# Where twelve modulation rows are loaded and summed in a decoder layer: convolution anchors, other buffers, three later sums

## The chip, the cores and the metric

The kernel runs on one core of a Trainium2 chip. The metric is device time in microseconds (us) for one execution of the whole layer. The engines of the core work side by side, each through its own list of instructions in a fixed order: PE (matrix products), DVE and POOL (elementwise), ACT (elementwise with functions; its queue also issues transfers), SP (issues transfers). An instruction that waits holds up all that stand behind it on its engine.

## The reference

One decoder layer for a sequence of 512 positions with 1024 channels, in float32. Cut to what matters here:

```python
mod = silu(c) @ ada_w + ada_b                       # c: 1024 -> 6 * 1024
sh1, sc1, g1, sh2, sc2, g2 = split(mod, 6)

u = rms_norm(x, mix_pre_g) * (1 + sc1) + sh1
qk_raw, v, o_pre, gates, glu = split(u @ w_in)
q, k = split(silu(causal_dwconv(qk_raw, width 4)))
h = mlstm_chunkwise(q, k, v, gates)                 # 4 heads of 256, chunks of 128
h = rms_norm(h, ml_norm_g) * sigmoid(o_pre)
y = silu(layer_norm(causal_dwconv(glu, width 31)))
mix = concat(h, y) @ w_out
x = x + g1 * rms_norm(mix, mix_post_g)

u = rms_norm(x, ffn_pre_g) * (1 + sc2) + sh2
a, gt = split(causal_dwconv(u @ ffn_up, width 3))
x = x + g2 * rms_norm((silu(gt) * a) @ ffn_down, ffn_post_g)
```

The change concerns `mod` alone: when its parts g1, sh2 and sc2 are computed, and from which buffers.

## The kernel before

**The products.** Every float32 matrix product is done as three products of rounded parts: a matrix is split into a high part (a rounding, on ACT, the names that end in h) and a low part, the remainder (a subtraction, on POOL or DVE, the names that end in l). `w_split` does this for the weights `wqko` and `wvo` of a head, `wo` of the output projection and `wup` of the FFN, 512 columns at a time. PE runs high x high, low x high and high x low.

**The stages.** In the opening x is normed and turned, and the first 16 modulation rows are made. Then the loop `for h in range(H - 1)` goes over heads 0 to 2: attention of head h is a generator `steps`, and between its steps head h+1 is projected. `head_proj(h + 1, i)` for i = 0 to 3 makes two tiles of q and two of k (`q_0c`, `q_1c`, `k_2c`, `k_3c`): products into a PSUM bank `qko`, then a convolution of four taps (the first on ACT, L562, three on DVE, L564) and a silu on ACT (L565). `make_vo(h + 1)` makes v and the output gate. `make_E(h + 1)` makes the decay matrices `E` with seven exps on ACT; DVE multiplies them with the scores `s` (L653). Calls of `pace()` in between run a part of the width-31 convolution (`cv`, `cs`). After the loop come attention of head 3 and the norm of the convolution branch (`ry_s` on PE, `ry_t` on DVE, `ry_r` on POOL), then the output projection by a scheme of few products (banks `mixa`, `mixb`; operands `mku`, `m`, `mt`, `ms`), and last the FFN with up and down projection, from about 400 us to the end.

**The modulation rows.** The 6144 values of `mod` are 48 rows of 128 values: row i is a tile of weights, 128 partitions x 1024, times silu(c) (in `cb`), summed along 1024. `ada_load(i)` issues the transfer of 512 KB on ACT's queue, and `ada_sum(i)` is one DVE instruction, a product with a running sum (L191, its output tile is called `junk`). Rows 0 to 15 are done in the opening. Rows 16 to 23 are g1, rows 24 to 39 are sh2 and sc2, and rows 40 to 47 are g2 and are done in the FFN. `ada_done(a, b)` adds the bias to a group of rows, and `gains` are worked out from it for the norms.

**Where rows are put.** A small pool `adas` has two buffers of one row. From row 24 on rows also go to other tiles that lie idle: four slots of `spare` (a large tile, free when the last projection of a head has been read), half tiles of a side buffer (30 and 31) and two wide tiles (34 and 35). A load has to wait for the sum that reads the row that was in the buffer before.

**What sets the order.** PE and SP run in the order of the program. ACT, DVE and POOL are ordered by a scheduler that simulates the kernel; `behind(ins, anchor)` pins an instruction behind another of the same engine, and `tc.cur_priority += LATER` lets it yield to others. Inside `with in_order():`, which holds the output projection, the order is again the program's. `last_e[0]` is the last tap issued, `last_left[0]` the last of a head's remainders.

Of the kernel before, what the change touches and what calls it, by code (L numbers as in the profile page):

```python
# [13 lines left out]
AF = mybir.ActivationFunctionType  # L14
# [3 lines left out]
P = 128  # L18
D = 1024
# [3 lines left out]
H = 4  # L23
# [34 lines left out]
def decoder_layer(ctx, tc, w_glu0, x, c, adaT, vecs, w_glu, w_qko, w_v0, w_vo, w_mq, w_out, w_up, w_down, out):  # L58
    nc = tc.nc
# [112 lines left out]

    def ada_load(i):

        if 24 <= i < 28 or i in (32, 33, 36, 37):
            q = 2 * (i % 4 if i < 36 else i - 34)
            r = spare[0][:, q : q + 2, :].rearrange("p j t -> p (j t)")
        elif 30 <= i < 32:
            if i % 2 == 0:
                spare.append(side(f"ada_{i}"))  # L180
            r = spare[-1][:, (i % 2) * D : (i % 2 + 1) * D]
        elif i in (34, 35):
            r = (wide1 if i == 34 else wide2)[:, :D]
        else:
            r = adas.tile([P, D], F32, tag="ada", name=f"ada_{i}")
        nc.scalar.dma_start(r, adaT[i // 2][:, (i % 2) * D : (i % 2 + 1) * D])
        ada_rows[i] = r

    def ada_sum(i):
        junk = small.tile([P, D], BF16, tag="junk", bufs=1, name=f"junk_{i}")  # L190
# [2 lines left out]
    def ada_block(i, anchor):  # L193
        ada_load(i)
        behind(ada_sum(i), anchor)
# [362 lines left out]
    def conv4(ps, i, name):  # L558

        t = slot(f"{name}c")  # L560
        w = lambda tap: vcol("qk_conv_w", tap * 16 + i)
        S.activation(t, ps, AF.Identity, bias=vcol("qk_conv_b", i), scale=w(3))  # L562
        for d in range(1, 4):
            last_e[0] = V.scalar_tensor_tensor(out=t[:, d:], in0=ps[:, : T - d], scalar=w(3 - d), in1=t[:, d:], op0=ALU.mult, op1=ALU.add)  # L564
        S.activation(t, t, AF.Silu)  # L565
        return t

    hy = [None] * (2 * KT)

    heads = {}  # L570
# [31 lines left out]
    last_left = [None]  # L602
# [131 lines left out]
        return [three[s][:, a : a + n] for (s, a), n in zip(PLACE, NS)]  # L734

    E = [None] * H

    LO = 32
    Mhl = const.tile([P, T], F32R, name="Mhl")
# [6 lines left out]
    def make_E(h):  # L746
        mb = atbank(f"Mb{h}")
        PE.matmul(mb, pick[:, h : h + 1].to_broadcast([P, P]), Mhl, start=True, stop=True)
        md = slot(f"Md{h}")
        V.tensor_tensor(out=md.rearrange("p (t m) -> p t m", t=NT), in0=mb.rearrange("p (t m) -> p t m", t=NT),  # L750
                        in1=cmask[:, None, :].to_broadcast([P, NT, P]), op=ALU.add)
        E[h] = head_tiles(f"E{h}", F32)
        for cc in range(NT):
            b = ga[:, cc, h : h + 1]
            S.activation(E[h][cc][:, :P], md[:, cc * P : (cc + 1) * P], AF.Exp, bias=b, scale=-1.0)
            if cc < NT - 1:
                S.activation(E[h][cc][:, P:], mb[:, (cc + 1) * P :], AF.Exp, bias=b, scale=-1.0)
    head_load(0)
    head_proj(0, 0)
    head_proj(0, 1)  # L760
# [193 lines left out]
    def pace():  # L954
        tc.cur_priority += LATER
        next(paced, None)
        tc.cur_priority -= LATER
# [33 lines left out]
    def norm_split(a, b):  # L991
        for j in range(a, b):
# [2 lines left out]
            last_yl[0] = V.tensor_tensor(out=lo, in0=ys[j], in1=hi.bitcast(F32), op=ALU.subtract)  # L995
            hy[KT + j] = (hi, lo)

    def ada_pair(i):
        tc.cur_priority += LATER
        for n in range(i, i + 2):  # L1000
            behind(ada_sum(n), last_e[0])
        tc.cur_priority -= LATER

    for h in range(H - 1):
        for i in range(16 + 2 * h, 18 + 2 * h):
            ada_load(i)
        head_load(h + 1)
        steps = attention(h)
        if h == 0:
            head_proj(1, 0)  # L1010
            ada_pair(16)
            next(steps)
            head_proj(1, 1)
            pace()
            next(steps)
            pace()
            head_proj(1, 2)
            pace()
            next(steps)
        else:  # L1020
            next(steps)
            ada_pair(16 + 2 * h)
            if h == H - 2:
                for i in range(22, 24):
                    ada_load(i)
            head_proj(h + 1, 0)
            pace()
            for _ in turns:
                pass
            head_proj(h + 1, 1)  # L1030
            pace()
            next(steps)
            pace()
            head_proj(h + 1, 2)
            pace()
            next(steps)
        head_proj(h + 1, 3)
        if h == H - 2:
            ada_pair(22)
            ada_done(16, 24)  # L1040
            gain(0, 16, "mix_post_g")
        values = make_vo(h + 1)
        pace()
        next(steps)
        pace()
        next(values)
        next(steps)
        pace()
        next(values)
        if h == 0:  # L1050
            next(steps)
            pace()
        make_E(h + 1)
        if h == H - 2:
            norm_mean()
        next(values)
        if h < H - 2:
            turns = steps
        else:
            for _ in steps:  # L1060
                pass
        next(values)
        if h == H - 2:
            norm_sums()
# [1 line left out]
    spare.append(upool.tile([P, KT, T], F32, tag="ul", name="spare"))  # L1066
    tc.cur_priority += LATER
    for i in range(24, 26):
        ada_block(i, last_left[0])
    for i in range(26, 30):  # L1070
        ada_load(i)
    tc.cur_priority -= LATER
# [93 lines left out]
    with in_order():  # L1166
        wt1 = right_split(wt1)
        for i in range(2):
            wo_split(r8, NP - 2, i)
        for _ in steps:  # L1170
            pass
        for i in range(35, 40):
            ada_sum(i)
        for p in range(PAIRS):
            mix_product("s1", wt1, banks[:2], p, True)
        for t, ps in zip(ku3, banks):
            V.tensor_tensor(out=t, in0=ps, in1=t, op=ALU.subtract)
        for t, ps in zip(ku2, banks):
            V.tensor_tensor(out=ps, in0=ps, in1=t, op=ALU.subtract)
        we = wo1_load(0, EARLY)  # L1180
        g1r = row(0, lambda n: [wide1[:, :T], wide1[:, T : 2 * T]], "g1", nc.sync)
        we = wo1_split(we, 0, EARLY)
        w22 = right_split(w22, slots, "t")
        for n in range(NP - 2, NP):
            mix_first(n)
        for n in range(EARLY):
            mix_plain(n, banks, we[n], (2, 3), n == 0)
        wo = wo1_split(wo1_load(EARLY, EARLY + 4), EARLY, EARLY + 4)
        for tt, ps in enumerate(mixa):
            V.tensor_tensor(out=mg[tt], in0=ps, in1=g1r[0], op=ALU.mult)  # L1190
            sq_sum(ps, msq[:, 2 * tt : 2 * tt + 1], f"mixa{tt}")
        for p in range(PAIRS):
            mix_product("s4", w22, banks[:2], p)
        for t, ps in zip(ku3, banks[2:]):
            V.tensor_tensor(out=ps, in0=ps, in1=t, op=ALU.add)
        for n in range(EARLY):
            mix_plain(n, banks, we[n], (0, 1))
        wo += wo1_split(wo1_load(EARLY + 4, NP), EARLY + 4, NP)
    ada_done(24, 40)
    V.scalar_tensor_tensor(out=gains[:, KT : 2 * KT], in0=sc2[:, :, 0], scalar=1.0, in1=vcols("ffn_pre_g", 0, KT), op0=ALU.add, op1=ALU.mult)  # L1200
    V.tensor_scalar(out=gains[:, KT : 2 * KT], in0=gains[:, KT : 2 * KT], scalar1=RD, scalar2=None, op0=ALU.mult)
# [477 lines left out]
```

## Time and profile before

| | |
|---|---|
| time before, median of 3 runs | 773.56 us (773.38 to 774.5) |
| the profiled execution | 773.63 us |
| its span, first to last instruction | 771.9 us |
| granted PE clock, mean | 0.998 of full speed |
| engines' busy share of the span | PE 98%, DVE 76%, POOL 71%, ACT 56% |
| bytes moved | 154.92 MB, mean 201 GB/s |
| modulation rows on ACT's queue, to the `ada` buffers | 22 transfers of 512 KB |
| sums of those rows | 22, 37.3 us of DVE, mean 1.70 us |

The span is what lies between the first and the last instruction recorded; the execution takes 1.7 us more. An engine's busy share is over the whole span. Idle time of DVE, ACT or POOL says little by itself, since PE has nearly none. In a row of the timeline stand the start in us, the duration, the engine, the line, the operation, and output<-inputs with their shapes; in brackets the engine's idle time just ahead and what ended it. "ACTq" is the issue of a transfer on ACT's queue. PE's waits are listed as us in total, number of times, and longest.

### The profile page before, as it was taken

How to read it: one execution, taken by the hardware profiler on the slowest of the kernel's cores; microseconds unless marked ns; L12 is line 12 of the kernel's file. 1: busy time of each engine (PE TensorE's matmuls, PEld its weight loads, DVE VectorE, ACT ScalarE, POOL GpSimd, SP SyncE). 2: the span in 40 equal slices, each digit the busy share in tenths (PEclk: the TensorE clock that was granted, in tenths of full speed). 3: DMA queues.
4: the chain of work that ended last, by engine and by line, in shares of the span. 5: the costliest groups of instructions: out<-in, count | busy, mean ns of one | idle time of the engine just before them, and what ended most of it. 6: DMA issues, size and time to landing. Idle time of an engine off the chain costs nothing.

```text
span 771.9 us, 10261 instructions
## 1 busy us (share of the span) xinstructions
PE 753.5 (98%) x3485; PEld 622.6 (81%) x3485; DVE 587.5 (76%) x866; ACT 428.5 (56%) x823; POOL 546.3 (71%) x443
## 2 busy tenths in 40 slices
PE   7999999999999989999999999999999999999996
PEld 5878898878777778778878988888888888888885
DVE  6769899989969986578978887774774776654547
ACT  7584429775745665485348644443445355566643
POOL 5789759995683962857931077886986885599943
PEclk9999999999999999999999999999999999999999
DMA  8994854231141233666663765857667474796263
GB/s 319 351 401 159 164 151 164 110 109 56 56 163 55 94 126 109 233 198 211 217 253 122 252 218 203 310 185 269 249 245 287 149 279 170 266 398 245 102 239 143
DMA packets 41976, 154.92 MB, mean 201 GB/s; under 512 B 3954, under 2 KB 5378, under 8 KB 32772
## 3 DMA queue, kind: packets, MB, share of 16 engines
q1 hardware_dynamic: 28052, 101.57, 36.5%
q10 hardware_dynamic: 12272, 49.56, 17.9%
q0 software_dynamic: 1600, 3.15, 2.4%
q8 instruction: 27, 0.44, 0.2%
q14 instruction: 25, 0.20, 0.1%
HBM read 134.19 MB, written 26.35 MB: 208 GB/s over the span
## 4 chain that ended last, share of the span: by engine, by line
PE 64%; DVE 15%; DMA 6%; POOL 5%; issue 5%; ACT 4%; DVEq 0%; SPq 0%; POOLq 0%; ACTq 0%
PE up L229 31%; PE dn L229 13%; PE glu L229 7%; DVE cv L917 6%; PE mixb L229 4%; DVE junk L191 3%; PE vo L229 3%; DMA wglu<-in_w_glu 3%; DMA spare<-in_adaT 2%; PE qko L229 1%; PE v L229 1%; POOL cs L913 1%; DMA wvo<-in_w_vo 1%; PE glu L366 1%; PE mixa L229 1%
## 5 line engine op out<-in xcount | busy, mean ns | idle before, releaser
L917 DVE SCALAR_TENSOR_TENSOR cv<-gt,cvw,cv 128x502 f32<-128x502 f32 (+23 forms) x200 | 136.7, 730 | 3.0 <-ACT cv L905 1.8
L913 POOL TENSOR_TENSOR cs<-cs,cs 128x510 f32<-128x510 f32 (+3 forms) x32 | 44.0, 1374 | 1.0 <-ACT cs L911 0.7
L191 DVE SCALAR_TENSOR_TENSOR junk<-ada,cb 128x1024 bf16<-128x1024 f32 x22 | 37.3, 1698 | 4.5 <-DMA ada<-in_adaT 4.2
L211 POOL TENSOR_TENSOR wup_0l<-wup,wup_0h 128x512 fp32r<-128x512 f32 x18 | 26.0, 1447 | 19.1 <-ACT wup_0h L210 19.1
L229 PE MATMUL up<-u2h,wup_1024h 128*128 128x512 f32 (+1 forms) x96 | 35.8, 373 | 0.0
L229 PE MATMUL up<-u2l,wup_512h 128*128 128x512 f32 (+1 forms) x96 | 35.7, 372 | 0.0
L229 PE MATMUL up<-u2h,wup_0h 128*128 128x512 f32 (+1 forms) x96 | 35.7, 372 | 0.0
L229 PE MATMUL up<-u2l,wup_0h 128*128 128x512 f32 (+1 forms) x96 | 35.7, 372 | 0.0
L229 PE MATMUL up<-u2h,wup_0l 128*128 128x512 f32 (+1 forms) x96 | 35.7, 372 | 0.0
L229 PE MATMUL up<-u2h,wup_1536l 128*128 128x512 f32 (+1 forms) x96 | 35.6, 371 | 0.0
L229 PE MATMUL up<-u2h,wup_512h 128*128 128x512 f32 (+1 forms) x96 | 35.6, 371 | 0.0
L229 PE MATMUL up<-u2h,wup_1536h 128*128 128x512 f32 (+1 forms) x96 | 35.6, 371 | 0.0
L229 PE MATMUL up<-u2l,wup_1536h 128*128 128x512 f32 (+1 forms) x96 | 35.6, 371 | 0.0
L229 PE MATMUL up<-u2h,wup_512l 128*128 128x512 f32 (+1 forms) x96 | 35.6, 371 | 0.0
L229 PE MATMUL up<-u2l,wup_1024h 128*128 128x512 f32 (+1 forms) x96 | 35.6, 371 | 0.0
L229 PE MATMUL up<-u2h,wup_1024l 128*128 128x512 f32 (+1 forms) x96 | 35.6, 371 | 0.0
L911 ACT ACTIVATE cs<-gt,cvw 128x511 f32<-128x511 f32 (+4 forms) x40 | 27.3, 714 | 11.3 <-POOL cs L913 6.2
L211 POOL TENSOR_TENSOR wup_1536l<-wup,wup_1536h 128x512 fp32r<-128x512 f32 x18 | 25.3, 1406 | 5.2 <-ACT wup_1536h L210 5.2
L1412 DVE TENSOR_TENSOR b<-b 128x512 f32<-128x512 f32 x11 | 19.4, 1762 | 9.4 <-POOL b L1411 9.4
L346 DVE SCALAR_TENSOR_TENSOR junk<-ada,cps 128x1024 bf16<-128x1024 f32 x16 | 19.5, 1220 | 8.7 <-DMA ada<-in_adaT 7.9
L1411 POOL TENSOR_TENSOR b<-b 128x512 f32<-128x512 f32 x11 | 14.7, 1334 | 15.3 <-DVE b L1410 15.3
L210 ACT ACTIVATE wup_512h<-wup 128x512 fp32r<-128x512 f32 x22 | 13.8, 627 | 19.8 <-POOL fq L1468 11.3
(1267 smaller groups left out, 2787.8 us busy)
## 6 DMA issues: line engine op xcount, KB each, us to landing
wup<-in_w_up SPq DMA_DIRECT2D x22, 1024.0 KB, 5.3
ada<-in_adaT ACTq DMA_DIRECT2D x22, 512.0 KB, 5.6
b<-in_w_down ACTq DMA_DIRECT2D x11, 1024.0 KB, 6.2
spill_t<-b ACTq DMA_DIRECT2D x11, 1024.0 KB, 4.0
wqko<-in_w_qko SPq DMA_DIRECT2D x9, 1024.0 KB, 4.7
ada<-in_adaT SPq DMA_DIRECT2D x16, 512.0 KB, 7.2
wvo<-in_w_vo SPq DMA_DIRECT2D x6, 1024.0 KB, 4.8
wglu<-in_w_glu SPq DMA_DIRECT2D x5, 1024.0 KB, 6.6
```

The source lines that it names most:

```text
L191: return V.scalar_tensor_tensor(out=junk, in0=ada_rows.pop(i), scalar=1.0, in1=cb, op0=ALU.mult, op1=ALU.mult, accum_out=mod[:, i : i + 1])
L210: S.activation(hi[:, :n], src, AF.Copy)
L211: last_w[0] = (eng or G).tensor_tensor(out=lo[:, :n], in0=src, in1=hi[:, :n].bitcast(F32), op=ALU.subtract)
L229: PE.matmul(ps, l, r, start=start and i == 0, stop=stop and i == 2, skip_group_check=again)
L346: V.scalar_tensor_tensor(out=junk, in0=first[k][:, i * D : (i + 1) * D], scalar=1.0, in1=cps, op0=ALU.mult, op1=ALU.mult, accum_out=part[: ...
L366: PE.matmul(ps, blk(wk, i)[a], u[k][b], start=k == 0 and p == 0, stop=k == KT - 1 and p == 1)
L911: S.activation(t[:, d:], cvx[j][:, : T - d], AF.Copy, scale=w(CK - 1 - d))
L913: G.tensor_tensor(out=side[:, d:], in0=side[:, d:], in1=t[:, d:], op=ALU.add)
L917: tap = V.scalar_tensor_tensor(out=cp[:, d:], in0=cvx[j][:, : T - d], scalar=w(CK - 1 - d), in1=cp[:, d:], op0=ALU.mult, op1=ALU.add)
L1411: G.tensor_tensor(out=b12, in0=b22, in1=b12, op=ALU.subtract)
L1412: V.tensor_tensor(out=b22, in0=b22, in1=b11, op=ALU.subtract)
```

## The change

Three things.

1. Rows 18 to 23. Each iteration of the loop loaded its own two rows, and the last iteration also rows 22 and 23, where the scheduler found them a place. Now each pair is loaded by `ada_next` behind the silu of a convolution: rows 18 and 19 behind that of `k_2c` in iteration 0, 20 and 21 behind that of `k_2c` in iteration 1, 22 and 23 behind that of `q_1c` in iteration 2.
2. Rows 24 and 25 are loaded to the two `adas` buffers, behind the last exp of head 3's `make_E`, not to `spare`. The slots of `spare` hold rows 26 to 29 now, and 36 to 39 after them; rows 32 and 33 take the `adas` buffers of 24 and 25.
3. The sums of rows 37 to 39 stand behind the last remainders of the output projection's weights, not ahead of its product `s1`. `ada_done(24, 40)` and the gains follow them.

```diff
--- before.py
+++ after.py
@@ -172,8 +172,8 @@
 
     def ada_load(i):
 
-        if 24 <= i < 28 or i in (32, 33, 36, 37):
-            q = 2 * (i % 4 if i < 36 else i - 34)
+        if 26 <= i < 30 or 36 <= i < 40:
+            q = 2 * ((i - 26) % 10)
             r = spare[0][:, q : q + 2, :].rearrange("p j t -> p (j t)")
         elif 30 <= i < 32:
             if i % 2 == 0:
@@ -183,8 +183,8 @@
             r = (wide1 if i == 34 else wide2)[:, :D]
         else:
             r = adas.tile([P, D], F32, tag="ada", name=f"ada_{i}")
-        nc.scalar.dma_start(r, adaT[i // 2][:, (i % 2) * D : (i % 2 + 1) * D])
         ada_rows[i] = r
+        return nc.scalar.dma_start(r, adaT[i // 2][:, (i % 2) * D : (i % 2 + 1) * D])
 
     def ada_sum(i):
         junk = small.tile([P, D], BF16, tag="junk", bufs=1, name=f"junk_{i}")
@@ -562,9 +562,10 @@
         S.activation(t, ps, AF.Identity, bias=vcol("qk_conv_b", i), scale=w(3))
         for d in range(1, 4):
             last_e[0] = V.scalar_tensor_tensor(out=t[:, d:], in0=ps[:, : T - d], scalar=w(3 - d), in1=t[:, d:], op0=ALU.mult, op1=ALU.add)
-        S.activation(t, t, AF.Silu)
+        last_silu[0] = S.activation(t, t, AF.Silu)
         return t
 
+    last_silu = [None]
     hy = [None] * (2 * KT)
 
     heads = {}
@@ -734,6 +735,7 @@
         return [three[s][:, a : a + n] for (s, a), n in zip(PLACE, NS)]
 
     E = [None] * H
+    last_exp = [None]
 
     LO = 32
     Mhl = const.tile([P, T], F32R, name="Mhl")
@@ -754,7 +756,7 @@
             b = ga[:, cc, h : h + 1]
             S.activation(E[h][cc][:, :P], md[:, cc * P : (cc + 1) * P], AF.Exp, bias=b, scale=-1.0)
             if cc < NT - 1:
-                S.activation(E[h][cc][:, P:], mb[:, (cc + 1) * P :], AF.Exp, bias=b, scale=-1.0)
+                last_exp[0] = S.activation(E[h][cc][:, P:], mb[:, (cc + 1) * P :], AF.Exp, bias=b, scale=-1.0)
     head_load(0)
     head_proj(0, 0)
     head_proj(0, 1)
@@ -995,6 +997,10 @@
             last_yl[0] = V.tensor_tensor(out=lo, in0=ys[j], in1=hi.bitcast(F32), op=ALU.subtract)
             hy[KT + j] = (hi, lo)
 
+    def ada_next(i):
+        for n in range(i, i + 2):
+            behind(ada_load(n), last_silu[0])
+
     def ada_pair(i):
         tc.cur_priority += LATER
         for n in range(i, i + 2):
@@ -1002,8 +1008,9 @@
         tc.cur_priority -= LATER
 
     for h in range(H - 1):
-        for i in range(16 + 2 * h, 18 + 2 * h):
-            ada_load(i)
+        if h == 0:
+            for i in range(16, 18):
+                ada_load(i)
         head_load(h + 1)
         steps = attention(h)
         if h == 0:
@@ -1015,23 +1022,25 @@
             next(steps)
             pace()
             head_proj(1, 2)
+            ada_next(18)
             pace()
             next(steps)
         else:
             next(steps)
             ada_pair(16 + 2 * h)
-            if h == H - 2:
-                for i in range(22, 24):
-                    ada_load(i)
             head_proj(h + 1, 0)
             pace()
             for _ in turns:
                 pass
             head_proj(h + 1, 1)
+            if h == H - 2:
+                ada_next(22)
             pace()
             next(steps)
             pace()
             head_proj(h + 1, 2)
+            if h < H - 2:
+                ada_next(20)
             pace()
             next(steps)
         head_proj(h + 1, 3)
@@ -1066,7 +1075,8 @@
     spare.append(upool.tile([P, KT, T], F32, tag="ul", name="spare"))
     tc.cur_priority += LATER
     for i in range(24, 26):
-        ada_block(i, last_left[0])
+        behind(ada_load(i), last_exp[0])
+        behind(ada_sum(i), last_left[0])
     for i in range(26, 30):
         ada_load(i)
     tc.cur_priority -= LATER
@@ -1169,7 +1179,7 @@
             wo_split(r8, NP - 2, i)
         for _ in steps:
             pass
-        for i in range(35, 40):
+        for i in range(35, 37):
             ada_sum(i)
         for p in range(PAIRS):
             mix_product("s1", wt1, banks[:2], p, True)
@@ -1196,6 +1206,8 @@
         for n in range(EARLY):
             mix_plain(n, banks, we[n], (0, 1))
         wo += wo1_split(wo1_load(EARLY + 4, NP), EARLY + 4, NP)
+        for i in range(37, 40):
+            ada_sum(i)
     ada_done(24, 40)
     V.scalar_tensor_tensor(out=gains[:, KT : 2 * KT], in0=sc2[:, :, 0], scalar=1.0, in1=vcols("ffn_pre_g", 0, KT), op0=ALU.add, op1=ALU.mult)
     V.tensor_scalar(out=gains[:, KT : 2 * KT], in0=gains[:, KT : 2 * KT], scalar1=RD, scalar2=None, op0=ALU.mult)
```

No instruction is added or removed on PE, DVE or POOL, and the order on PE and SP stays as it was; on POOL two neighbouring instructions change places. On ACT, iteration 2, where rows 22 and 23 (`ada_2692`, `ada_2694`) were loaded between the roundings of a weight; `q_0c` is the first tap of head 3's first convolution. Before:

```order
L210 ACTIVATE wvo_0_0h<-wvo_0_2902 128x512
L210 ACTIVATE wvo_0_512h<-wvo_0_2902 128x512
L186 DMA ada_2692<-in_adaT 128x1024
L210 ACTIVATE wvo_0_1024h<-wvo_0_2902 128x512
L186 DMA ada_2694<-in_adaT 128x1024
L210 ACTIVATE wvo_0_1536h<-wvo_0_2902 128x512
L562 ACTIVATE q_0c<-qko_0_2696,vec 128x512
```

The two loads stand between the roundings of `wvo_0`. After, the same place on ACT:

```order
L210 ACTIVATE wvo_0_0h<-wvo_0_2902 128x512
L210 ACTIVATE wvo_0_512h<-wvo_0_2902 128x512
L210 ACTIVATE wvo_0_1024h<-wvo_0_2902 128x512
L210 ACTIVATE wvo_0_1536h<-wvo_0_2902 128x512
L562 ACTIVATE q_0c<-qko_0_2692,vec 128x512
```

They are gone from there. Further on ACT, around the silu of `q_1c` (L565), the loads are called `ada_2796` and `ada_2798`:

```order
L925 ACTIVATE gt_771<-cv_2366 128x512
L565 ACTIVATE q_1c<-q_1c 128x512
L187 DMA ada_2796<-in_adaT 128x1024
L187 DMA ada_2798<-in_adaT 128x1024
L562 ACTIVATE k_2c<-qko_2_2808,vec 128x512
```

The loads moved from between the roundings to behind the silu of `q_1c`.

On DVE, at the start of head 3's attention, the sums of rows 24 and 25, with `ms` the last remainder, `ry_t` of the branch's norm and the products of `E` with the scores. Before:

```order
L617 SCALAR_TENSOR_TENSOR ms_2_3090<-hT_1_3077,ghalf,ms_2_3091 128x256
L248 TENSOR_SCALAR ry_t<-ry_s 128x4
L653 SCALAR_TENSOR_TENSOR E_3022<-s_0_3195,E_3022 128x512
L191 SCALAR_TENSOR_TENSOR junk_3137,mod<-spare,cb 128x1024
L653 SCALAR_TENSOR_TENSOR E_3023<-s_1_3199,E_3023 128x384
L191 SCALAR_TENSOR_TENSOR junk_3140,mod<-spare,cb 128x1024
```

Each sum stands between two `E`s here. After, the same place on DVE:

```order
L618 SCALAR_TENSOR_TENSOR ms_2_3090<-hT_1_3077,ghalf,ms_2_3091 128x256
L191 SCALAR_TENSOR_TENSOR junk_3138,mod<-ada_3136,cb 128x1024
L191 SCALAR_TENSOR_TENSOR junk_3142,mod<-ada_3140,cb 128x1024
L248 TENSOR_SCALAR ry_t<-ry_s 128x4
L654 SCALAR_TENSOR_TENSOR E_3022<-s_0_3195,E_3022 128x512
L654 SCALAR_TENSOR_TENSOR E_3023<-s_1_3199,E_3023 128x384
```

The two sums read the small pool's buffers and stand ahead of `ry_t` and of the first `E`.

On DVE, in the output projection, the sums of rows 36 to 39 and the first use of the banks behind the products of `s1`. Before:

```order
L191 SCALAR_TENSOR_TENSOR junk_3677,mod<-spare,cb 128x1024
L191 SCALAR_TENSOR_TENSOR junk_3679,mod<-spare,cb 128x1024
L191 SCALAR_TENSOR_TENSOR junk_3681,mod<-ada_3633,cb 128x1024
L191 SCALAR_TENSOR_TENSOR junk_3683,mod<-ada_3635,cb 128x1024
L1177 TENSOR_TENSOR mku_3358<-mixb_3621,mku_3358 128x512
L1177 TENSOR_TENSOR mku_3359<-mixb_3622,mku_3359 128x512
L1179 TENSOR_TENSOR mixb_3621<-mixb_3621,mku_3286 128x512
```

Four sums stand ahead of `mku`. After, the same place on DVE:

```order
L191 SCALAR_TENSOR_TENSOR junk_3677,mod<-spare,cb 128x1024
L1187 TENSOR_TENSOR mku_3358<-mixb_3623,mku_3358 128x512
L1187 TENSOR_TENSOR mku_3359<-mixb_3624,mku_3359 128x512
L1189 TENSOR_TENSOR mixb_3623<-mixb_3623,mku_3286 128x512
L1189 TENSOR_TENSOR mixb_3624<-mixb_3624,mku_3287 128x512
```

One sum is left there. Further on DVE, at the last remainders of `wo` and the first of `wup`:

```order
L211 TENSOR_TENSOR wo_8l<-wo_6_3823,wo_8h 128x512
L211 TENSOR_TENSOR wo_9l<-wo_6_3823,wo_9h 128x512
L191 SCALAR_TENSOR_TENSOR junk_3841,mod<-spare,cb 128x1024
L191 SCALAR_TENSOR_TENSOR junk_3843,mod<-spare,cb 128x1024
L191 SCALAR_TENSOR_TENSOR junk_3845,mod<-spare,cb 128x1024
L211 TENSOR_TENSOR wup_0l<-wup_3852,wup_0h 128x512
L211 TENSOR_TENSOR wup_512l<-wup_3852,wup_512h 128x512
```

Three sums moved from ahead of `mku` to behind `wo_9l`, ahead of the FFN's first remainders.

## The prediction

> **What bounds the kernel now.** I read the engines' totals first, then what PE (the matrix engine) waited for, then the end of the run by windows, and last the timeline around each wait that the change touches. All rows are of the one profiled execution, which took 773.63 us; the median of the runs is 773.56, so 0.07 comes off at the end. In the first fence stand the engines' busy times, then PE's waits (us in total, times, longest), then one window (us, busy time of PE, PE's loads, DVE, ACT and POOL, clock, DMA share, GB/s).
>
> ```profile
> PE 753.5 (98%) x3485; PEld 622.6 (81%) x3485; DVE 587.5 (76%) x866; ACT 428.5 (56%) x823; POOL 546.3 (71%) x443
> ...
> PE qko L229 <- DVE q_0c L564: 2.4, 1, 2.4
> PE s L652 <- DVE E L653: 1.6, 1, 1.6
> PE mixb L229 <- DVE mixb L1179: 1.5, 1, 1.5
> PE qko L229 <- DVE ms L617: 1.1, 1, 1.1
> ...
> PE o L663 <- ACT hn L667: 0.8, 1, 0.8
> PE mixa L229 <- ACT mku L889: 0.6, 1, 0.6
> ...
> 387.40:760.00 372.60, 372.59 (x1749) 312.51 (x1750) 253.19 (x327) 194.43 (x354) 256.68 (x206) 1.00 0.64 232
> ```
>
> PE is busy 98% of the span, at full clock, and from 387.40 to 760.00 it is busy 372.59 of 372.60 us. The matmuls are the same in both kernels, and in the same order on PE. So a change can shorten this kernel only by closing one of the gaps on PE, and each us so closed is a us of the end, because the work behind 387.40 is PE and nothing else. Six single waits between 220 and 388 make 8.0 us. The question for each part of the change is which of these it takes away, and whether it opens one.
>
> **Part 1, rows 18 to 23 (the gap of 2.42).** Timeline rows: start, duration, engine, line, operation; in brackets the idle time ahead and what ended it.
>
> ```profile
> 267.03 0.61 ACT L210 ACTIVATE wvo_512h<-wvo 128x512 fp32r<-128x512 f32 x1
> ...
> 267.51 2.06 DVE L191 SCALAR_TENSOR_TENSOR junk<-ada,cb 128x1024 bf16<-128x1024 f32 x1
> ...
> 269.61 0.33 ACTq L186 DMA_DIRECT2D ada<-in_adaT  x1
> 269.61 2.20 DVE L191 SCALAR_TENSOR_TENSOR junk<-ada,cb 128x1024 bf16<-128x1024 f32 x1
> ...
> 269.99 0.63 ACT L210 ACTIVATE wvo_1024h<-wvo 128x512 fp32r<-128x512 f32 x1 [2.34 <-DVE junk L191]
> ...
> 272.23 0.63 ACT L210 ACTIVATE wvo_1536h<-wvo 128x512 fp32r<-128x512 f32 x1 [1.61 <-DVE junk L191]
> ...
> 272.77 0.77 ACT L562 ACTIVATE q_0c<-qko,vec 128x512 f32<-128x512 f32 x1
> ...
> 273.57 0.75 DVE L564 SCALAR_TENSOR_TENSOR q_0c<-qko,vec,q_0c 128x511 f32<-128x511 f32 x1 [1.75 <-ACT q_0c L562]
> ...
> 276.79 0.74 DVE L564 SCALAR_TENSOR_TENSOR q_0c<-qko,vec,q_0c 128x509 f32<-128x509 f32 x1
> ...
> 277.68 0.47 PE L229 MATMUL qko<-uh,wqko_0h 128*128 128x512 f32 x1 [2.42 <-DVE q_0c L564]
> ```
>
> The load of row 22 stands on ACT's queue between two weight roundings and needs the buffer of row 20, so ACT stands still until DVE has summed row 20 (267.51+2.06); row 23 does the same behind row 21. ACT loses 2.34+1.61 us, its q_0c starts at 272.77, and DVE, done with row 21 at 271.82, idles 1.75 until that q_0c has begun to come out. PE then waits 2.42 for DVE's third tap, since it needs the bank that the taps read.
>
> With the two loads moved behind the silu of a later convolution, ACT goes straight on: 267.03 + 3 roundings of about 0.55 each puts q_0c near 268.7, and the first tap then waits for DVE alone, at 271.82. That is 1.75 of the 2.42; the other 0.67 is DVE's own queue (two sums ahead of the taps) and stays. The bounds are 0 (something else holds ACT or DVE there) and 2.42. I take 1.75, since DVE's idle row gives just what is removed. Where the loads stand now, behind a silu that follows the taps, the sums of rows 20 and 21 are done, so ACT waits for nothing new. The issues of rows 18 to 21 move by the same rule, past the roundings of their iteration; each takes 0.33 us of ACT's queue, no compute, and the rows are still loaded an iteration before their sums. I put these at nothing.
>
> **Part 2, rows 24 and 25 (the gap of 1.59).**
>
> ```profile
> 308.12 0.40 ACT L755 ACTIVATE E<-Md,ga 128x128 f32<-128x128 f32 x1
> ...
> 314.41 0.48 DVE L617 SCALAR_TENSOR_TENSOR ms<-hT,ghalf,ms 128x256 f32<-128x256 f32 x1
> ...
> 317.09 0.82 ACTq L186 DMA_DIRECT2D spare<-in_adaT  x2
> ...
> 317.87 0.16 DVE L248 TENSOR_SCALAR ry_t<-ry_s 128x4 f32<-128x4 f32 x1 [2.97 <-PE ry_s L235]
> ...
> 319.69 0.69 DVE L653 SCALAR_TENSOR_TENSOR E<-s,E 128x512 f32<-128x512 f32 x1 [1.66 <-PE s L652]
> ...
> 322.26 1.01 POOL L250 TENSOR_TENSOR ry_r<-ry_t,mhalf 128x4 f32<-128x4 f32 x1
> ...
> 324.23 1.36 DVE L191 SCALAR_TENSOR_TENSOR junk<-spare,cb 128x1024 bf16<-128x1024 f32 x1 [3.85 <-DMA spare<-in_adaT]
> ...
> 326.13 0.49 PE L652 MATMUL s<-q_0c,k_2c 128*128 128x128 f32 x2 [1.59 <-DVE E L653]
> ```
>
> Rows 24 and 25 wait for the spare tile, which is free only at 317.09; they land 7.1 us later, and DVE, which has the sum of row 24 between two of head 3's E products, idles 3.85 us for it although the scores of the second E are there. PE waits 1.59 for that E. In the changed kernel both rows go to the small pool's buffers, are issued behind the last exp (308.12+0.40), and their sums stand right behind the last remainder (314.41+0.48), ahead of ry_t. What lands when, and how long a sum takes, comes from these two rows (count: min/median/max ns; then us to landing):
>
> ```profile
> L191 DVE SCALAR_TENSOR_TENSOR junk<-ada,cb x22: 1212/1708/2198, 160.8 to 461.7; 128x1024 bf16<-128x1024 f32 x22
> ...
> DMA to landing us min/median/max: 4.0/6.7/13.6
> ```
>
> Issued at 308.5 and landing at the median of 6.7, the row is there at 315.2. Two sums of 1.21 to 2.20 end at 317.6 to 319.6, and ry_t, now due at 317.87, is up to 1.7 late. The scores that the first E reads come at 319.69 (1.66 idle on DVE for them), so E is not late. The late ry_t goes to ry_r on POOL, which started it only at 322.26, long after 317.87+0.16, so it was not DVE that POOL waited for; 4.2 us of cover. Neither sum now stands between E products: the gain is the 1.59. Bounds: 1.59, or with a landing at 13.6 (322.1) the sums end at 324.5 to 326.5, then come ry_t and the first E, 0.16+0.69, and the second E starts at 325.4 to 327.4; it started at 324.23+1.36 = 325.59 before, so the gap stays as it was or grows by 1.8. The median lies far inside, so I take 1.59.
>
> [...]
>
> **Part 3, the last three sums (the gap of 1.48).**
>
> ```profile
> 376.51 2.20 DVE L191 SCALAR_TENSOR_TENSOR junk<-spare,cb 128x1024 bf16<-128x1024 f32 x1
> ...
> 377.33 0.39 PE L229 MATMUL mixb<-mt_2h,ms 128*128 128x512 f32 x1
> ...
> 383.21 2.19 DVE L191 SCALAR_TENSOR_TENSOR junk<-ada,cb 128x1024 bf16<-128x1024 f32 x1
> ...
> 384.28 2.26 POOL L211 TENSOR_TENSOR m_2l<-m,m_2h 128x512 fp32r<-128x512 f32 x1
> ...
> 386.54 1.28 DVE L1179 TENSOR_TENSOR mixb<-mixb,mku 128x512 f32<-128x512 f32 x2
> ...
> 387.37 0.47 PE L229 MATMUL mixb<-m_0h,ms 128*128 128x512 f32 x1 [1.48 <-DVE mixb L1179]
> ...
> 393.66 0.68 DVE L211 TENSOR_TENSOR wo_9l<-wo,wo_9h 128x512 fp32r<-128x512 f32 x1
> ...
> 397.01 0.69 DVE L211 TENSOR_TENSOR wup_0l<-wup,wup_0h 128x512 fp32r<-128x512 f32 x1 [2.66 <-ACT wup_0h L210]
> ...
> 400.69 0.21 DVE L834 TENSOR_SCALAR rm0t<-msq 128x1 f32<-128x1 f32 x1 [1.18 <-ACT mixb0junk L827]
> ```
>
> Before, DVE sums rows 36 to 39 (376.51 to 385.40) ahead of mku and mixb, though PE had finished what mku reads at 377.72. Three of the four leave: 3 x 2.19 = 6.6 us. mixb would then be ready near 380, and PE reaches it at 387.37-1.48 = 385.89. The gap of 1.48 is covered four times: gain 1.48.
>
> The three sums are now behind wo_9l. DVE gets there earlier, by up to 393.66+0.68-6.6 = 387.8; wo's weights may hold it, so I estimate 389.6. Three sums of 1.21 to 2.20 end at 393.2 to 396.2. The next on DVE is wup_0l, which waits for ACT and began at 397.01 after 2.66 idle, so they fit the hole: cost 0. The other end: DVE is no earlier than before (394.34), the sums end at 400.9, the four up remainders (0.6 each) and the gains follow to 403.9, and rm0t, at 400.69-1.48 = 399.2 in the shifted run, is 4.6 late, on the path to the FFN's first matmuls. Net of the gain this is -3.1. I take 0, nearer by DVE's 2.66 idle row and the 6.6 us that have left it.
>
> **Sum.** 1.75 + 1.59 + 1.48 = 4.82 off 773.63 is 768.81; less 0.07, **768.8**. The gaps of 1.14, 0.82, 0.64 and those of the opening stay.
>
> **Rivals.**
>
> (B) More than that: the load of head 2's second weight also comes in faster.
>
> ```profile
> 215.92 7.79 DMA wvo<-in_w_vo
> ...
> DMA to landing us min/median/max: 4.7/4.8/5.2
> ...
> 228.11 0.75 DVE L564 SCALAR_TENSOR_TENSOR q_1c<-qko,vec,q_1c 128x511 f32<-128x511 f32 x1 [4.29 <-ACT q_1c L562]
> ```
>
> The chain has 7.79 us for this load, where most of that tile's take 4.8 to the landing. Two modulation rows were issued 4 us ahead of it; moved to a later convolution, they are out of its way. If it lands 3 us earlier, ACT is about 2.4 earlier at q_1c, the 4.29 of idle on DVE shrinks, and 0.82 (at hn) and the 0.67 left at place 1 go too: 768.8-1.5 = 767.3. [...]
>
> (C) One of the three terms isn't paid: ACT or DVE is held by something else at place 1, or the last sums are late. Without one term 770.3 to 770.6.
>
> (N) The change doesn't do what it says: the waits reappear one instruction on, and PE closes under 1.5 us in all: about 773.
>
> (D) Slower: rows 24 and 25 land late. Their sums stand in DVE's queue ahead of ry_t and all of head 3's E products, while PE waits for the scores' E. A landing at 13.6 costs up to 1.8 there, which parts 1 and 3 (3.23) still outweigh. To end 1.55 later than before, part 2 must lose 3.23+1.55 = 4.78, 3.0 more than that: it decides from a landing 16.6 us after the issue (325.1), and each us beyond is a us of the end, above 775.1. The longest seen was 13.6.
>
> **Chances.** A as summed 0.48; B 0.25; C 0.15; N 0.08; D 0.04. The range takes A and B with their bounds and C: from B less 0.5 for a further gap, 766.8, to C's upper end plus 0.4, 771.0. What a measurement of this kernel can tell from no change is about 0.2%, 1.55 us: faster means below 772.0 (A, B, C: 0.88), the same is N (0.08), slower D (0.04).
>
> **What would show it.** Part 1 right: ACT's four roundings stand without a pause and PE's wait at 277.7 is under 0.8. Part 2: sums of rows 24 and 25 begin by 316.5, ahead of ry_t, and PE has no wait for E of head 3. Part 3: one sum ahead of mku, PE runs through 385.9, three sums end before ACT's wup_0h. B: that wvo load takes about 5 us. Wrong would be a new PE wait at rm0t or behind 387, where there was none, or a wait for ry_b near 329.

## The result and the profile after

The changed kernel took 767.52 us (median, 766.41 to 769.35) beside 773.47 for the kernel before: ratio 0.9927, 95% interval 0.9899 to 0.9955. Measured once more beside the experiments, it took 766.94 beside 771.89 for the kernel before: ratio 0.9935 (0.9913 to 0.9958). The forecast was 768.8. Two executions further down, of 1485 us (part 1 alone) and 841 us (without part 1), ran slow at a granted clock of 0.91 and 0.85; they are in the medians of their kernels and not in the ratios.

The profiled execution took 766.63 us, its span 764.9. All that PE waited for in it (us in total, times, longest), then the first product that stood behind the wait for mixb, then a window from just behind it to 753, and last two windows of the opening:

```profile
PE cps L161 <- ACT crow L160: 2.9, 1, 2.9
PE glu L366 <- ACT uh L387: 1.7, 1, 1.7
PE qko L229 <- DVE ms L618: 1.1, 1, 1.1
PE mixa L229 <- ACT mku L891: 0.2, 1, 0.2
...
380.48 0.39 PE L229 MATMUL mixb<-m_0h,ms 128*128 128x512 f32 x1
...
381.30:753.00 371.70, 371.70 (x1747) 311.73 (x1746) 252.29 (x326) 191.56 (x348) 253.51 (x204) 1.00 0.64 232
...
12.89:16.30 3.41, 1.66 (x8) 1.00 (x7) 3.10 (x8) 2.84 (x6) 1.99 (x3) 1.00 1.03 415
16.30:19.71 3.41, 3.41 (x14) 2.91 (x13) 3.38 (x7) 1.55 (x3) 2.69 (x3) 0.50 0.90 308
```

Of the six waits between 220 and 388 two are left, 1.14 almost as it was (1.10) and 0.64 shrunk to 0.2: 8.1 us became 1.3. The opening, which the change doesn't touch, is worse: PE waits 1.75 for `uh`, where it was 1.10, and behind that wait the granted clock is 0.50 for 3.41 us.

PE runs its 3485 products in the same order in both profiles, so each can be set beside its like. The starts of the products behind the six waits, in us:

| product behind the wait for | before | after | earlier by |
|---|---|---|---|
| ms, at 220 | 220.46 | 221.21 | -0.75 |
| hn | 233.75 | 233.54 | 0.21 |
| q_0c | 277.68 | 274.70 | 2.98 |
| E | 326.13 | 321.42 | 4.71 |
| mku | 343.33 | 338.09 | 5.24 |
| mixb | 387.37 | 380.48 | 6.89 |
| (the last product) | 765.33 | 758.34 | 6.99 |

So between these two executions each wait that went comes to the end in full; 0.75 is lost ahead of them, in the opening. But the waits at hn and E, 2.7 us of the 7.0, belong to the one profile of the kernel before: in none of the other thirteen, with the change or with parts of it, is there one above 0.2.

The three places in the timeline after:

```profile
267.11 0.63 ACT L210 ACTIVATE wvo_1536h<-wvo 128x512 fp32r<-128x512 f32 x1 [0.79 <-PE qko L229]
267.65 0.77 ACT L562 ACTIVATE q_0c<-qko,vec 128x512 f32<-128x512 f32 x1
267.78 2.19 DVE L191 SCALAR_TENSOR_TENSOR junk<-ada,cb 128x1024 bf16<-128x1024 f32 x1
...
269.90 0.74 DVE L564 SCALAR_TENSOR_TENSOR q_0c<-qko,vec,q_0c 128x511 f32<-128x511 f32 x1
...
313.32 2.20 DVE L191 SCALAR_TENSOR_TENSOR junk<-ada,cb 128x1024 bf16<-128x1024 f32 x1
...
314.40 2.25 POOL L211 TENSOR_TENSOR mt_1l<-mt,mt_1h 128x512 fp32r<-128x512 f32 x1
...
315.45 0.15 DVE L248 TENSOR_SCALAR ry_t<-ry_s 128x4 f32<-128x4 f32 x1
...
316.73 0.69 DVE L654 SCALAR_TENSOR_TENSOR E<-s,E 128x512 f32<-128x512 f32 x1 [1.13 <-PE s L653]
...
374.36 1.28 DVE L1187 TENSOR_TENSOR mku<-mixb,mku 128x512 f32<-128x512 f32 x2
...
385.39 1.21 DVE L191 SCALAR_TENSOR_TENSOR junk<-spare,cb 128x1024 bf16<-128x1024 f32 x1
...
387.91 1.22 DVE L191 SCALAR_TENSOR_TENSOR junk<-spare,cb 128x1024 bf16<-128x1024 f32 x1
389.06 0.69 DVE L211 TENSOR_TENSOR wup_0l<-wup,wup_0h 128x512 fp32r<-128x512 f32 x1
...
393.70 0.21 DVE L836 TENSOR_SCALAR rm0t<-msq 128x1 f32<-128x1 f32 x1 [1.78 <-ACT mixb0junk L829]
```

ACT's roundings run on to q_0c, but for 0.79 in which the last one waits for PE; the first tap follows the sums on DVE with no idle time. The sums of rows 24 and 25 stand ahead of ry_t and E still waits for PE's scores, 1.13. DVE turns to mku at 374.36, and the last three sums take 1.21 to 1.23 each, with POOL idle, and end ahead of rm0t with 1.78 to spare. They end at 389.13 and not, as the prediction's sign had it, before ACT's wup_0h, which began at 388.01; PE has no wait from it.

### The profile page after: what moved, and what is told of

It is laid out like the page before. It is cut to its first block, busy times and chain, and to the rows that moved or that the text cites. A ratio compares the mean times of both kernels' runs of the same rounds, so it can differ in the third digit from the quotient of the medians.

```text
span 764.9 us, 10251 instructions
## 1 busy us (share of the span) xinstructions
PE 752.8 (98%) x3485; PEld 623.8 (82%) x3485; DVE 584.2 (76%) x866; ACT 428.1 (56%) x823; POOL 542.8 (71%) x443
## 4 chain that ended last, share of the span: by engine, by line
PE 82%; DVE 6%; POOL 4%; ACT 3%; issue 3%; DMA 1%; DVEq 0%; SPq 0%; ACTq 0%; POOLq 0%
PE up L229 31%; PE dn L229 13%; PE glu L229 7%; PE vo L229 6%; PE mixa L229 5%; PE mixb L229 5%; PE glu L366 4%; PE qko L229 4%; DVE cv L919 3%; PE o L664 2%; PE v L229 1%; POOL cs L915 1%; PE s L653 1%; DMA wglu<-in_w_glu 1%; ACT cs L913 1%
## 5 line engine op out<-in xcount | busy, mean ns | idle before, releaser
L211 POOL TENSOR_TENSOR wup_512l<-wup,wup_512h 128x512 fp32r<-128x512 f32 x18 | 24.7, 1372 | 0.0
```

The lines of the kernel that those rows point to most:

```text
L211: last_w[0] = (eng or G).tensor_tensor(out=lo[:, :n], in0=src, in1=hi[:, :n].bitcast(F32), op=ALU.subtract)
```

## The experiments

Ratios are to runs of the kernel before on the same chip, beside the same experiments. Its medians there were 770.60, 771.89 and 772.04 in the three sets, and single executions lay between 767.7 and 776.2.

**1. One part alone.** Four kernels: the before with part 1, with only the loads of rows 22 and 23, with part 2, with part 3.

```diff
 # part 3 alone
-        for i in range(35, 40):
+        for i in range(35, 37):
             ada_sum(i)
...
         wo += wo1_split(wo1_load(EARLY + 4, NP), EARLY + 4, NP)
+        for i in range(37, 40):
+            ada_sum(i)
```

> Part 1 alone (loads of rows 18 to 23 behind the later silus; rows 24, 25 and the last three sums as before). Theory B (rows 20 and 21 had slowed head 2's wvo load): that load lands in about 5 us, the waits of 2.42 at q_0c and 0.82 at hn both go, time 3.0 to 3.4 us under before; the 1.59 and 1.48 stay. Theory A (the slow landing was chance and nothing but ACT's two waits counts): 1.75 under before, 0.7 of the wait at q_0c and the 0.82 at hn stay.

> Only the loads of rows 22 and 23 moved (18 to 21 at the iterations' starts as before). Theory A: the wait at q_0c falls from 2.42 to 0.67 (or to 0 if DVE is early), time 1.75 to 2.4 under before. Theory B: the same 1.75 here, and head 2's wvo load still takes over 6 us with the 0.82 at hn in place. If the slow landing was chance, that load takes about 5 us here too and the 0.82 is gone.

> Part 2 alone (rows 24 and 25 in the small pool's buffers, loaded behind the last exp). The sum's term: the wait of PE for E of head 3, 1.59, goes: 1.6 under before. If ACT's mku (0.64) was held by the six loads to the spare tile, of which four are left ahead of it, up to 0.45 more: 2.0. [...]

> Part 3 alone (sums of rows 37 to 39 behind wo_9l). The sum's term: the wait for mixb, 1.48, goes and nothing comes behind it: 1.5 under before. Rival: the sums hold the first up remainders or rm0t, and PE waits behind 390: 0 to 3 slower than before.

| kernel | median, us | ratio to before (95%) |
|---|---|---|
| part 1 | 770.92 | 0.9993 (0.9971 to 1.0015) |
| rows 22 and 23 only | 770.49 | 1.0005 (0.9984 to 1.0026) |
| part 2 | 771.09 | 1.0000 (0.9977 to 1.0023) |
| part 3 | 767.99 | 0.9969 (0.9946 to 0.9991) |

Parts 1 and 2 alone gained nothing that can be measured. Both theories had this wrong for part 1; for part 2 the sum's term of 1.6 was wrong, and experiment 2 shows why. Part 3 alone gained 2.6 us by the medians, more than its term of 1.5. The waits that parts 1 and 2 aim at were gone all the same. PE's waits in the profile of part 1 alone, then a sum and POOL's remainder beside it, then two windows, the first DVE's stretch up to mixb, the second the 3.8 us that follow the wait:

```profile
PE mixb L229 <- DVE mixb L1187: 2.6, 1, 2.6
PE qko L229 <- DVE ms L618: 1.1, 1, 1.1
...
370.33 1.29 POOL L211 TENSOR_TENSOR wo_0l<-wo,wo_0h 128x512 fp32r<-128x512 f32 x1
370.41 2.29 DVE L191 SCALAR_TENSOR_TENSOR junk<-wide,cb 128x1024 bf16<-128x1024 f32 x1
...
356.69:382.80 26.11, 24.35 (x112) 19.80 (x110) 25.84 (x29) 10.60 (x20) 25.96 (x14) 1.00 0.58 194
...
383.20:387.00 3.80, 3.40 (x9) 2.76 (x10) 3.80 (x8) 2.23 (x7) 3.29 (x3) 0.56 0.02 4
```

The same stretch and the same pair of instructions in the kernel before:

```profile
375.25 1.21 DVE L191 SCALAR_TENSOR_TENSOR junk<-wide,cb 128x1024 bf16<-128x1024 f32 x1
375.26 2.36 POOL L211 TENSOR_TENSOR wo_0l<-wo,wo_0h 128x512 fp32r<-128x512 f32 x1 [0.19 <-ACT wo_0h L210]
...
361.53:386.54 25.01, 24.35 (x112) 19.80 (x110) 24.73 (x29) 10.62 (x20) 24.77 (x13) 1.00 0.61 202
```

The stretch begins 4.84 us earlier than before, as much as the waits of 2.42, 0.82 and 1.59 that this execution no longer had. So what was closed further up did reach DVE; it was lost in the stretch and behind it. DVE runs the same 29 instructions almost without a pause in both, and with part 1 they take 1.10 longer, nearly all of it one sum: 2.29 instead of 1.21, where POOL began its remainder 0.08 ahead of it and not 0.01 behind. The wait for mixb is then 2.56 and not 1.48, and with that the granted clock falls to 0.56 for the next 3.8 us: 9 products, where the kernel without part 3 below did 15 in 4.0. All three profiles with rows 22 and 23 moved and the sums in their old place have this wait at 2.46 to 2.56; the two without that move have 1.5. The mean granted clock was at most 0.997 in each of 11 executions of part 1 alone; of 35 executions of the kernel before it was 0.998 or more in 17.

And there was less to gain than the one profile of the kernel before had it. With part 3 alone, which changes nothing ahead of 376, PE's wait at place 1 was

```profile
PE qko L229 <- DVE q_0c L564: 0.6, 1, 0.6
```

and it had none at hn or E. So the wait at place 1 also differs from one execution to the next: 2.42 here, 2.04 in the profile of part 2 alone, 0.60 in this one, though ACT stood at the two loads in all three. From this came theory C, that parts 1 and 2 count only with part 3.

**2. One part left out**, to test theory C.

> The whole change once more, on the chip and beside the runs on which its parts are timed. Theory C (the last three sums carry the change; the other two parts gain only because the sums no longer stand behind them): all of PE's waits between 250 and 390 under 0.5 each, time at or a little under that of the last three sums alone, 0.5 to 1.0 us under it. Theory A (three terms that add): 4.8 under the kernel before.

> Parts 2 and 3 without part 1 (rows 18 to 23 as before). Theory C: within 1 us of the whole change, with a wait at q_0c of 0.6 to 2.4 left, as the transfers fall out. Theory A: 1.75 slower than the whole change.

> Parts 1 and 3 without part 2 (rows 24 and 25 in the spare tile). Theory C: within 0.5 us of the whole change, since the wait for E was seen in the one profiled execution of before only; mku's wait back at 0.4 to 0.6. Theory A: 1.6 slower than the whole change, with PE's wait for E of head 3 in the profile.

> Parts 1 and 2 without part 3 (the last three sums ahead of mku). Theory C: the time of the kernel before within 1 us; PE's waits at q_0c, hn, E gone and the one for mixb at 387 grown to 2.5 or more, with a lower granted clock on PE in the 4 us behind it. Theory A: 3.3 under the kernel before, with the wait for mixb at its 1.5.

| kernel | median, us | ratio to before (95%) |
|---|---|---|
| whole change | 766.94 | 0.9935 (0.9913 to 0.9958) |
| without part 1 | 768.69 | 0.9955 (0.9933 to 0.9977) |
| without part 2 | 766.67 | 0.9932 (0.9906 to 0.9958) |
| without part 3 | 769.53 | 0.9974 (0.9954 to 0.9994) |

By the medians the whole change is 4.95 us under the kernel before, theory A's 4.8. Theory C has its waits right, none above 0.2 between 250 and 390, but its time (0.5 to 1.0 under part 3 alone) only if medians of two sets are compared (1.05); by the ratios it is 2.6. Without part 1 it is 1.75 slower, theory A's number again; without part 2 theory C is right; without part 3 neither is. By the scatter of the runs these differences from the whole change are good to 1.4, 0.8 and 1.1 us. The profile without part 1 doesn't show where its 1.75 goes: theory C's wait at q_0c isn't in it, and PE, held by a wait of 2.47 for ms at 221.6, comes to q_0c 2.0 later than in the changed kernel.

Part 2 is worth nothing that can be measured in the time. Six kernels of these experiments keep rows 24 and 25 in the spare tile, and in none of their profiles does PE wait for E. The reason is the load. In the kernel without part 2 (issue, and the sum that waits for it):

```profile
313.49 0.33 ACTq L187 DMA_DIRECT2D spare<-in_adaT  x1
...
318.79 1.23 DVE L191 SCALAR_TENSOR_TENSOR junk<-spare,cb 128x1024 bf16<-128x1024 f32 x1 [2.00 <-DMA spare<-in_adaT]
```

From issue to sum it is 5.3 us here, 4.7 to 5.8 in the other five, and 7.1 in the profile that the prediction was made from. The wait of 1.59 belonged to that execution. What part 2 does show is PE's wait for mku: 0.17 to 0.19 in the seven profiles with it, 0.19 to 0.65 in the seven without.

Without part 3 the kernel gained 0.26%, more than theory C's "time of the kernel before", less than theory A's 3.3 us. The wait for mixb is there as theory C has it, but the clock did not fall in the profiled execution. Its window, and for comparison the window behind a wait as long (2.47, at ms, in the kernel without part 1):

```profile
382.67 0.47 PE L229 MATMUL mixb<-m_0h,ms 128*128 128x512 f32 x1 [2.46 <-DVE mixb L1189]
...
382.00:386.00 4.00, 3.33 (x15) 2.76 (x16) 4.00 (x8) 2.16 (x7) 3.57 (x3) 1.00 0.02 4
```

```profile
221.59 0.47 PE L229 MATMUL qko<-uh,wqko_0h 128*128 128x512 f32 x1 [2.47 <-DVE ms L617]
...
221.60:224.00 2.40, 2.40 (x9) 1.92 (x10) 2.40 (x5) 1.96 (x4) 2.40 (x3) 0.79 0.00 0
224.00:226.00 2.00, 2.00 (x6) 1.61 (x5) 0.95 (x3) 1.99 (x3) 2.00 (x3) 0.50 0.78 254
```

So a wait of about 2.5 us sometimes costs half the clock and sometimes nothing; where it does, PE's products behind it come 1.4 to 1.6 us later than by the wait alone. Waits of 2.42 (place 1 before) and of 1.48 cost none. The traces show a difference between the two sorts. The granted clock changes in them at steps of 3.41 us (in the change's profile at 16.30, 19.71 and 763.82; the last is 218 steps of 3.413 behind the second). Counted from the span's start, this grid lies 0.38 us behind a whole number of steps in the profile of the kernel before, 2.65 in the change's, 0.83 with part 1 alone and 3.18 without part 3. A spell at 0.50 ahead of PE's last product lasts one step: 16.30 to 19.71 in the change's profile, 383.12 to 386.53 with part 1 alone. Here are two neighbouring steps around the wait for mixb, first in the profile of part 1 alone, then in the one without part 3:

```profile
379.71:383.12 3.41, 1.33 (x6) 0.75 (x5) 3.41 (x5) 0.00 (x0) 3.41 (x3) 1.00 0.00 0
383.12:386.53 3.41, 2.93 (x7) 2.38 (x8) 3.41 (x8) 1.79 (x5) 3.37 (x3) 0.50 0.02 5
...
378.65:382.06 3.41, 1.56 (x7) 0.94 (x6) 3.41 (x5) 0.00 (x0) 3.41 (x3) 1.00 0.00 0
382.06:385.47 3.41, 2.80 (x12) 2.35 (x13) 3.41 (x7) 1.66 (x5) 3.41 (x3) 1.00 0.02 5
```

With part 1 alone PE is idle for 2.08 of a step, and the next step runs at half the clock. Without part 3 the grid cuts the wait in two, 1.85 and 0.61, and the clock stays. The other cases behind the opening agree: 2.01 (without part 1, at ms) and 2.06 (rows 22 and 23 only, at mixb) idle in one step are followed by 0.50, while 1.77 (part 2 alone, the wait of 2.04) and 1.60 (before, the wait of 2.42) are not. In the opening 1.67, 1.75 and 1.99 were followed by 0.50 and 1.51 was not; why less idle time did it there is open.

Of theory C this stands: with the four sums ahead of mku, part 1 is offset by a wait at mixb that is 1 us longer and that, as the grid falls, can have half the clock behind it (0.50 with part 1 alone, 1.00 without part 3).

**3. Which rows of part 1, and how free is the new place of the sums.**

> Part 3 with the loads of rows 22 and 23 moved (18 to 21 as before, 24 and 25 in the spare tile). Theory C1 (ACT standing at the loads of rows 22 and 23 is what part 1 removes): the wait at q_0c is gone, time within 0.6 us of parts 1 and 3 together, that is 0.6 to 0.7% under the kernel before. Theory B (rows 18 to 21 ahead of head 2's weight load count): that load lands 5 to 8 us after its issue, PE's wait at hn is there in some executions, 0.8 to 1.5 us slower than parts 1 and 3.

> Part 3 with the loads of rows 18 to 21 moved (22 and 23 still between the roundings). Theory C1: no better than part 3 alone, 0.3% under the kernel before, with a wait at q_0c or ms of 0.6 to 2.5 near 275. Theory B: head 2's weight load lands in 5.1 to 5.4 us, DVE is earlier, and the wait at q_0c falls under 0.7: 0.5 to 0.6% under the kernel before.

> The whole change with three more sums of the same size (their result is not used) behind sum 39. Prediction's term (the place behind wo_9l is free): in the profile of the whole change DVE idles 1.78 us ahead of rm0t, so of 3 x 1.22 = 3.7 us 1.8 are hidden and rm0t is 1.9 late: PE waits about 1.9 for it and the time is 1.9 over the whole change. Rival (PE has cover behind mixb): no wait, time as the whole change.

| kernel | median, us | ratio to before (95%) |
|---|---|---|
| part 3, rows 22 and 23 | 767.40 | 0.9944 (0.9923 to 0.9965) |
| part 3, rows 18 to 21 | 767.43 | 0.9940 (0.9920 to 0.9959) |
| whole change and three more sums | 768.78 | 0.9955 (0.9937 to 0.9974) |

Each half of part 1 comes to 0.25 or 0.3% over part 3 alone, both to 0.37% (the kernel without part 2); the intervals don't tell the halves apart. For rows 18 to 21 that is theory B's 0.5 to 0.6% under the kernel before and not C1's 0.3%; for rows 22 and 23 it is a little less than C1's 0.6 to 0.7%. The profiles show what each does. With rows 18 to 21 in their old place, head 2's weight load came in, from its issue to the first rounding that waits for it, after 7.87, 6.34, 4.97, 5.81, 4.98 and 6.98 us in six profiles; with them moved, after 5.14 to 5.39 in eight. Issue and rounding in the profile of the kernel before and of the change:

```profile
215.92 0.33 SPq L218 DMA_DIRECT2D wvo<-in_w_vo  x1
...
223.79 0.63 ACT L210 ACTIVATE wvo_0h<-wvo 128x512 fp32r<-128x512 f32 x1 [5.54 <-DMA wvo<-in_w_vo]
```

```profile
216.67 0.33 SPq L218 DMA_DIRECT2D wvo<-in_w_vo  x1
...
221.92 0.64 ACT L210 ACTIVATE wvo_0h<-wvo 128x512 fp32r<-128x512 f32 x1 [2.92 <-DMA wvo<-in_w_vo]
```

That agrees with rival B: where the two rows are issued some 4 us ahead of the weight, it comes in later than 5.39 in four of six profiles, by up to 2.5 us. Only the latest of them, 7.87, is followed by a wait at hn. With rows 22 and 23 alone moved the wait at q_0c was 0.5, with 18 to 21 alone 0.9, with neither 0.6, with both 0; single waits of this size are not enough to split the gain.

The three more sums cost 1.8 us by the medians (0.2%, 1.5 us, by the ratios; the whole change was measured in another set). rm0t came at 395.41, right behind them, 1.5 later than in the changed kernel after allowing for 0.2 that this profile ran late, but PE did not wait for it at once:

```profile
PE xT L1264 <- ACT un L1256: 0.6, 2, 0.4
PE up L229 <- ACT u2h L1286: 0.4, 1, 0.4
PE up L229 <- DVE u2l L1290: 0.3, 1, 0.3
```

Four waits of 1.3 in all, behind rm0t's followers, and PE's products behind them are 2.0 later than in the changed kernel for it. So the forecast of 1.9 was about right, by waits at other places than rm0t. The place is free for the three sums and not for six.

**4. The last wait.** In the changed kernel ACT stands at a copy of the width-31 convolution, ahead of q_0c of head 2, and PE then waits 1.10 for ms. The copy is put behind `mh`:

```diff
+            if h == 1:
+                behind(side_ins[6, 5], last_mh[0])
             head_proj(h + 1, 1)
```

Here `side_ins[6, 5]` is that copy and `last_mh[0]` the rounding `mh` of the left parts (L616). The orders of PE, DVE, POOL and SP are the same.

> The whole change, and one copy of the width-31 convolution (cs_5 of its seventh tile, which holds ACT for 2.24 us until POOL's ysq) behind the left parts mh of head 1 on ACT, so that q_0c of head 2 starts 3 us earlier. If ACT standing there is what PE's last wait of 1.1 (for ms, at 220) comes from: that wait goes, 1.1 us under the whole change. Rival: POOL or DVE hold ms anyway, or the late copy holds POOL's additions; no change, or the wait comes back at the next convolution.

It took 764.86 us (764.29 to 766.29), ratio 0.9905 (0.9884 to 0.9925), beside 766.94 for the change alone: the fastest kernel here. Its profile, the copy in the change first, then in this kernel ACT's q_0c and the copy, and PE's waits behind the opening:

```profile
215.43 0.72 ACT L913 ACTIVATE cs<-gt,cvw 128x507 f32<-128x507 f32 x1 [2.24 <-POOL ysq L939]
```

```profile
212.78 0.76 ACT L562 ACTIVATE q_0c<-qko,vec 128x512 f32<-128x512 f32 x1
...
215.08 0.73 ACT L915 ACTIVATE cs<-gt,cvw 128x507 f32<-128x507 f32 x1
...
PE mixa L229 <- ACT mku L893: 0.2, 1, 0.2
PE qko L229 <- DVE q_0c L564: 0.2, 1, 0.2
```

The wait of 1.1 is gone and 0.2 came at q_0c. By the medians, which are of two sets, the gain is 2.1, by the ratios 0.3%, and between the two profiles 1.8. Product by product, 0.9 of this is the wait moved as forecast. The other 0.9 is the opening, where this profile has a wait of 1.04 for `uh` and full clock, and the changed kernel's 1.75 and the spell at half clock; that is not the copy's doing.

## Why the prediction was right or wrong

**The time** was in the range, by a sum whose terms were not, and that is luck: part 2's 1.59 is not in the time, and part 3 gave about 1 us more than its 1.48. At each of the three places the wait named went. At q_0c and mixb it went by the mechanism named; at E it is gone without part 2 too.

**"Each us so closed is a us of the end"** holds between the two profiles: from row to row of the table above a closed wait brings 0.1 to 0.35 more than its idle time. It failed as a rule for adding terms that are read from one execution. Alone, parts 1 and 2 gave 0.0 to 0.07% and part 3 0.31%; left out of the whole, part 1 costs 1.75 us (1.5 by the ratios), part 2 nothing (-0.3) and part 3 2.6. The wait at mixb was taken as fixed, and it is not: work that moves ahead of it changes which DVE sum meets which POOL remainder, by 1.1 us, and a longer wait can lower the clock of what follows (0.56 in the 3.8 us behind the wait of 2.56).

**Part 1's term**, 1.75, agrees with what leaving it out costs, but what it is made of is only in part known. Rows 22 and 23 free ACT as foretold. Rows 18 to 21, put at nothing, gave 0.29% over part 3 by themselves, and with them moved head 2's weight load always came in within 5.39 us, which is rival B's, a quarter of the chance. How the time divides between the two the runs don't tell. The 0.67 said to stay went too, and the 0.82 at hn belonged to that execution.

**Part 2's term**, 1.59, was 0. The step took a landing of 7.1 us from a single execution for the kernel's own; the usual one leaves PE no wait there. In their new place the second of the two sums took 2.20 and POOL's mt_1l beside it 2.25, where in the profile before, with no sum beside it, mt_1l took 1.27. With that ry_r lost 1.0: POOL began mt_1l 2.9 earlier than before and ry_r, at 320.34, 1.9 earlier. The 4.2 us of cover held, and no wait for ry_b came. Where such a meeting did matter is a place that the prediction didn't look at, sum 35 in experiment 1: there the one that started first took 1.21 us (the sum, before) or 1.29 (the remainder, with part 1 alone), and the other 2.36 or 2.29.

**Part 3's term**, 1.48, was 2.4 to 2.6 by the medians. Its wait is 1.48 when sum 35 gets by POOL and about 2.5 when not, and about 2.5 can cost the clock as well: with 2.06 or 2.08 us of it in one step of 3.41 the next step ran at 0.50, with 1.85 at 1.00. The cost of the sums' new place was 0 as taken. Its other end, a rm0t "on the path" late by 4.6 and priced at 4.6, did not come; the three more sums, with rm0t 1.5 late and 2.0 lost on PE, show that the price was about right.

**Rivals N and D** did not occur: no wait for ry_b or rm0t came, and rows 24 and 25 were there when their sums' turn came.

Between the two profiles the gain is divided by the table above. How much of it is the clock and how much the waits over all executions stays open, since only the changed kernel has two profiles, and the shares differ from one execution to the next.

## What to carry to other kernels

When PE is nearly always busy, ask of each closed gap what PE meets next: where a helper engine works without a pause up to a later meeting point, the gain is safe only when that stretch is made shorter too. Size a wait that ends on a transfer by more than one execution. Count a long wait for more than its length: behind the opening, 2.01 to 2.08 us of idle time in one step of 3.41 were followed here by a step at 0.50, which cost 1.4 to 1.6 us more, and where the steps lay differed from one profiled execution to another.

## What the runs showed of the hardware that I had not expected

- The granted clock changed at steps of 3.41 us, on a grid that lay 0.38, 2.65, 0.83 and 3.18 us behind a whole number of steps (of 3.413) from the span's start in four executions. Two waits of PE of the same 2.46 to 2.47 us: one (mixb, without part 3) had 1.85 of it in one step and the clock stayed at 1.00, the other (ms, without part 1) 2.01 and the next step ran at 0.50.
- Sum 35 on DVE, begun 0.01 us ahead of the POOL remainder beside it, took 1.21 us and the remainder 2.36 (before); begun 0.08 us behind it, 2.29 and the remainder 1.29 (part 1 alone).
